# Hybrid diffusion backbone layer on one core: rows of h staged through the weight ring, layer-norm rows loaded one by one

## The chip, the core and the metric

The kernel runs on one core of a Trainium2 chip. The core has a matrix engine (PE in the profile; PEld is its weight load), a vector engine (DVE), a scalar engine (ACT), GpSimd (POOL) and a sync engine (SP), which here only issues DMAs. Each of them takes its own instructions strictly in the order in which they were put on its queue, and waits on semaphores for the others. 16 DMA engines move the data. The metric is the device time of one execution in microseconds; smaller is better.

## The reference, cut to what matters

One layer over 256 latent tokens `x` and 256 context tokens `ctx`, width 2048, all in float32:

```python
mod = silu(c) @ w_mod + b_mod;  shift, scale, gate = split(mod, 3)       # and the same for c_ctx
h   = layer_norm(x)   * (1 + scale)   + shift
h_c = layer_norm(ctx) * (1 + scale_c) + shift_c
aq, ak, av, az, bq, bk, bv, bz, bg, mga, mgb = split(h @ w_in)           # h_c: ak, av, bk, bv, bg are used
y_a = neighborhood_attention(aq, ak, av, ak_c, av_c, na_rpb)             # 16 heads of 64
y_b = gla(bq, bk, bv, bg, bk_c, bv_c, bg_c)                              # 4 heads, both directions
out = (sigmoid(mga) * ((y_a*silu(az)) @ w_br_a)
       + sigmoid(mgb) * ((y_b*silu(bz)) @ w_br_b)) @ w_out
x   = layer_norm(2**0.25 * x + gate * out, ln_g, ln_b)
```

## The kernel before, in words

**Number format.** Each factor of the big products is split into a high and a low part in the matrix engine's replicated float32 format (`split`, L146): ACT casts the high part (L148), DVE subtracts it from the source to get the low part (L150). Three matmuls (high x high, high x low, low x high) replace one.

**The weight ring.** All weights come as loads of 128 x 1024 numbers (512 KB; 352 KB for the value columns) through one tag of tiles, `raw`, with four buffers (`load`, L155, DMA at L157 on SP). A load's raw buffer is free again when its L150 has ended. The two parts go to tags `hi` and `lo` with three buffers each, which are free when the matmuls that read them are done. Two other things use the same four `raw` buffers: the position-bias tiles `rb` of the attention (L510, held from their fetch until both score blocks have added them), and the tiles `hr` with rows of h (L800, held until the four groups of matmuls that read them). Loads are counted from 1 in program order: loads 1 to 12 are aq0, aq1 (two each) and the eight value loads av0; 13 to 24 and 25 to 36 the same for the next two pairs of heads; 37 to 42 aq6, ak7, aq7; 43 to 50 bk and bq of the first GLA head.

**Rows of h.** The matrix engine needs h in two layouts. The transposed one is made at the start and stays on the chip (`hl`, tag of one buffer). The other one, token rows in two parts, is made in eight steps n = 0 to 7 (`rows_of_h`, L410) and stored to DRAM (`hrows`), from where `attended` reads it back as `hr` (L801). One step: SP loads the modulation columns, broadcast over the partitions, from DRAM `mods` into `sb` (L417) and rows of x into `xr` (L418); DVE makes h of them in eight instructions (four L423, four L424), ACT casts the high part into `sb`, DVE writes the low part over `xr` (L148, L150), SP stores both (L437). `sb` and `xr` are the two buffers of tag `staging`, so step n + 1 can't load before the stores of step n have ended. After step 6 in program order the tables `cs` and `wg` of the GLA stage take the same two buffers; `wg` is last read by the gates of head 3, `cs` by the rotation of its queries.

**What sets the order.** Program order is a priority. Steps hang on the loads as events (L444 to L451): the fetch of step n on load 6 + 6n, its cast and low part on the load behind it, its stores on load 11 + 6n. `tc.issue_after(ins)` puts an instruction behind `ins` on the queue of the engine of `ins`. A planner at build time walks through the program with estimated durations, gives out the buffers and writes each engine's fixed queue: an instruction whose buffer or input isn't there yet in its estimate lets later ones of the same engine pass.

**Attention's evacuation.** After the two query projections of a pair of heads, each 128 x 512 accumulator `qp` is emptied in eight short instructions that alternate between ACT (L495, L499) and DVE (L496, L500); the value projection `va` needs four accumulators of the same tag (`acc`, four buffers), so its third and fourth wait for the last L500 of either projection.

**The end.** When the last product that reads `hl` is done, its memory becomes `tail` (L1021): the rows of x, the layer-norm rows ln_g and ln_b (`fin`, four slices of 1 MB), the gate row and the results. The four slices are loaded by four DMAs on POOL's queue (L1033, L1034). The output projection `wo` runs in 24 loads (three column groups of eight) and a held last group; `turn` at the seventh load of the first group transposes the last quarter of the merged branches (`mt`, L934).

Of the kernel before, what the change touches and what calls it, by code (L numbers as in the profile page):

```python
# [8 lines left out]
F32 = mybir.dt.float32  # L9
# [7 lines left out]
P = 128  # L17
# [71 lines left out]
def tile_backbone_layer(  # L89
# [21 lines left out]
    nc = tc.nc  # L111
    const = ctx.enter_context(tc.tile_pool(name="const", bufs=1))
    hpool = ctx.enter_context(tc.tile_pool(name="hpool", bufs=1))
    stream = ctx.enter_context(tc.tile_pool(name="stream", bufs=3))
# [4 lines left out]
    mods = dram.tile([KT, 4, P], F32, name="mods")  # L119
# [11 lines left out]
    def acc(name):  # L131
        return ps.tile([P, 512], F32, tag="acc", name=name, bufs=4)
# [13 lines left out]
    def split(hi, lo, src, after=None):  # L146
        with tc.issue_after(after[0]) if after else nullcontext():
            cast = nc.scalar.copy(hi, src)  # L148
        with tc.issue_after(after[1]) if after else nullcontext():
            sub = nc.vector.tensor_tensor(out=lo, in0=src, in1=hi.bitcast(F32), op=ALU.subtract)  # L150
        return cast.ins, sub.ins

    loads, events = [], {}

    def load(src, n, name, after=None):  # L155
        raw = stream.tile([P, 1024], F32, tag="raw", name=f"r_{name}", bufs=4)
        dma = nc.sync.dma_start(raw[:, :n], src).ins  # L157
        hi = stream.tile([P, 1024], F32R, tag="hi", name=f"h_{name}")
        lo = stream.tile([P, 1024], F32R, tag="lo", name=f"l_{name}")
        cast, sub = split(hi[:, :n], lo[:, :n], raw[:, :n], after)  # L160
        loads.append((cast, sub))
        for event in events.pop(len(loads), ()):
            event(dma, sub)
        return hi, lo

    def unit(name, k):
        return load(wst[UNIT_AT[name, k]], 1024, f"{name}_{k}")
# [183 lines left out]
    for kt in range(KT):  # L351
# [3 lines left out]
        for p in range(K0):  # L355
# [3 lines left out]
            c = slice(P * p, P * p + P)  # L359
# [47 lines left out]
    def staging(shape, name, dt=F32R):  # L407
        return const.tile(shape, dt, tag="staging", name=name, bufs=2)

    def rows_of_h(n):  # L410
        sb = staging([P, 2, 4, P], f"sb{n}")
        xr = staging([P, 2, 4, P], f"xr{n}")
        b, x = sb[:].bitcast(F32), xr[:].bitcast(F32)

        def fetch_and_scale(dma, sub):
            with tc.issue_after(dma):
                nc.sync.dma_start(b, mods[2 * n : 2 * n + 2].partition_broadcast(P))  # L417
                nc.sync.dma_start(x, xrow[n])  # L418
            for i in range(4):
                xi, s = x[:, :, i, :], i // 2  # L420
                scale, shift = (b[:, :, 2 * m + s, :] for m in range(2))
                with tc.issue_after(sub):
                    nc.vector.scalar_tensor_tensor(xi, xi, mvs[:, i, 0:1], scale, ALU.subtract, ALU.mult)  # L423
                nc.vector.scalar_tensor_tensor(xi, xi, rsn[:, 0, i : i + 1], shift, ALU.mult, ALU.add)  # L424

        def parts(dma, sub):
            with tc.issue_after(sub):
                split(
                    sb[:].rearrange("p a b c -> p (a b c)"),
                    xr[:].rearrange("p a b c -> p (a b c)"),  # L430
                    x.rearrange("p a b c -> p (a b c)"),
                )

        def store(dma, sub):
            with tc.issue_after(dma):
                for part, src in enumerate((b, x)):
                    nc.sync.dma_start(  # L437
                        hrows[2 * n : 2 * n + 2, :, part].rearrange("f p j c -> p f (j c)"),
                        src.rearrange("p f a b -> p f (a b)"),
                    )  # L440

        return fetch_and_scale, parts, store

    for n in range(8):  # L444
        events.setdefault(6 + 6 * n, []).append(lambda dma, sub, n=n: rows_event(n, dma, sub))

    def rows_event(n, dma, sub):
        fetch, parts, store = rows_of_h(n)
        fetch(dma, sub)
        events.setdefault(7 + 6 * n, []).insert(0, parts)  # L450
        events.setdefault(11 + 6 * n, []).insert(0, store)  # L451
# [153 lines left out]
    for g in range(3):  # L605
# [4 lines left out]
        n = len(loads) + 1  # L610
# [13 lines left out]
    n = len(loads)  # L624
# [20 lines left out]
    lo = slice(64, 128)  # L645
# [283 lines left out]
    def turned(name, s, half):  # L929
        tp = bank(f"{name}_{half}")  # L930
        for i in range(2):
            for t in range(2):
                o = 256 * half + P * i
                nc.tensor.transpose(tp[:, T * i + P * t : T * i + P * t + P], s[:, t, o : o + P], ident[:])  # L934
        return tp
# [41 lines left out]
    def gated(c, which, ah, al, kt):  # L977
        g = rows_of(f"mg{which}{c}", xh, xl)
        s = k4([P, 2, 512], f"s{which}{c}")
        for t in range(2):  # L980
            sig = nc.scalar.activation(s[:, t, :], g[t][:], AF.Sigmoid)
        p = rows_of(f"p{which}{c}", ah, al, kt)
        for t in range(2):
            nc.vector.tensor_tensor(out=s[:, t, :], in0=s[:, t, :], in1=p[t][:], op=ALU.mult)
        return s, sig

    def turn(c, s):
        for half in range(2):
            tp = turned(f"mt{c}", s, half)
            a = 4 * c + 2 * half  # L990
            split(
                mhs[a // 8][:, a % 8 : a % 8 + 2, :].rearrange("p a b -> p (a b)"),
                mls[a // 8][:, a % 8 : a % 8 + 2, :].rearrange("p a b -> p (a b)"),
                tp[:],
            )
# [10 lines left out]
    for c in range(NC):  # L1006
# [5 lines left out]
        sb, sig = gated(c, "b", ybh, ybl, KT)  # L1012
# [9 lines left out]
    fin, gb, zs, zt0 = tail[:, 0:4], tail[:, 4], (tail[:, 5], tail[:, 6]), tail[:, 7]  # L1022
# [3 lines left out]
    for g in range(4):  # L1026
# [3 lines left out]
        mm(bp[:], ones_r[:], gh[:], True, False)  # L1030
        mm(bp[:], ones_r[:], gl[:], False, True)
        nc.scalar.copy(gb[:, 512 * g : 512 * g + 512], bp[:])
    for i, src in enumerate((xin[0], xin[1], lng.partition_broadcast(P), lnb.partition_broadcast(P))):  # L1033
        nc.gpsimd.dma_start(fin[:, i, :], src)  # L1034
    x_in, ln_g, ln_b = fin[:, 0:2], fin[:, 2], fin[:, 3]
    eps = tiny([P, 1], "eps", 1)
    nc.gpsimd.memset(eps[:], 1e-6)
# [4 lines left out]
    def out_mm(dst, wh, wl, a, t):  # L1042
        mh = mhs[a // 8][:, a % 8, P * t : P * t + P]
        ml = mls[a // 8][:, a % 8, P * t : P * t + P]
        mm(dst, mh, wh, a == 0, False)
        mm(dst, mh, wl, False, False)
        return mm(dst, ml, wh, False, a == KT - 1)

    def residual(op, t, n, lo, hi, scaled):
        cols = slice(lo, hi)  # L1050
        z = zs[t][:, cols]
        nc.vector.tensor_tensor(out=z, in0=op, in1=gb[:, cols], op=ALU.mult)
        nc.vector.scalar_tensor_tensor(z, x_in[:, t, cols], ALPHA, z, ALU.mult, ALU.add)
        nc.vector.bn_stats(sts[t][:, n, :], z)
        if scaled is not None:
            scaled.tensor_tensor(out=z, in0=z, in1=ln_g[:, cols], op=ALU.mult)

    for g in range(NC - 1):
        ops = [acc(f"wo{g}_{t}") for t in range(2)]
        for k in range(0, KT, 2):  # L1060
            if g == 0 and k == 12:
                turn(NC - 1, merged)
            wh, wl = unit(f"wo{g}", k)
            for t in range(2):
                for i in range(2):
                    c = slice(512 * i, 512 * i + 512)
                    out_mm(ops[t][:], wh[:, c], wl[:, c], k + i, t)
        for t in range(2):
            residual(ops[t][:], t, g, 512 * g, 512 * g + 512, nc.gpsimd)

    last = []
    for u in range(8):
        src = wst[UNIT_AT[f"wo{NC - 1}", 2 * u]]
        if u < HELD:
            raw = stream.tile([P, 1024], F32, tag="raw", name=f"r_last{u}", bufs=4)
# [4 lines left out]
        elif u == HELD:  # L1080
            raw = stream.tile([P, 1024], F32, tag="raw", name=f"r_last{u}", bufs=4)
# [163 lines left out]
```

## Time and profile before

| | us |
|---|---|
| median of 3 runs | 1234.91 (1233.46 to 1236.47) |
| the profiled execution's own time | 1236.99 |
| its span (first to last instruction) | 1235.3 |
| granted clock of the matrix engine, mean | 0.996 |
| bytes moved | 263.45 MB, mean 213 GB/s |

The profile's timeline gives, for each run of like instructions, the start, the time from the start of the first to the end of the last, the engine, the line and the operands; in brackets stands how long the engine was idle before it and on what it waited. A line of SP is the issue of a DMA. In the views by stage the columns are the busy time of PE, PEld, DVE, ACT and POOL with the number of instructions, the granted clock, the share of the DMA engines' time and GB/s.

### The profile page before, as it was taken

The numbers are of one execution on the slowest core, as the hardware profiler recorded it, in microseconds if no ns is written. First come the engines' busy times: TensorE is split into PE (matmuls) and PEld (weight loads), VectorE is DVE, ScalarE is ACT, GpSimd is POOL, SyncE is SP. The second block draws the span as 40 slices with busy tenths as digits, with TensorE's granted clock in tenths as the row PEclk, the third lists the DMA queues.
The fourth block names the chain that finished last, engine by engine and source line by source line (L and its number), as shares of the span: only waits on it lengthen the run. The fifth ranks groups of instructions, "written<-read, shape, count | busy, mean of one in ns | idle before, by whom it ended". The sixth has DMA issues, their size and how long they took to land.

```text
span 1235.3 us, 16298 instructions
## 1 busy us (share of the span) xinstructions
PE 1201.4 (97%) x6233; PEld 991.1 (80%) x6233; DVE 774.2 (63%) x1154; ACT 544.8 (44%) x776; POOL 65.9 (5%) x91
## 2 busy tenths in 40 slices
PE   6999999989999999999999999999999999999997
PEld 4666798979887887888888888888888888888785
DVE  6755677657759486355643466766566665665577
ACT  4322455545555354253532374544444444454341
POOL 1000100000001111001000000000000000000111
PEclk9999999999999999999999999999999999999999
DMA  9998566656743433543645567677776767657661
GB/s 372 417 404 308 160 199 187 201 169 189 237 144 109 135 126 130 188 153 120 238 165 189 213 226 233 231 235 239 238 247 230 241 237 241 227 187 268 215 216 68
DMA packets 77054, 263.45 MB, mean 213 GB/s; under 512 B 8920, under 2 KB 8936, under 8 KB 71856
## 3 DMA queue, kind: packets, MB, share of 16 engines
q1 hardware_dynamic: 73040, 252.49, 59.1%
q0 software_dynamic: 3504, 9.36, 2.7%
q8 instruction: 49, 0.80, 0.3%
q10 hardware_dynamic: 432, 0.56, 0.1%
q14 instruction: 29, 0.24, 0.1%
HBM read 247.66 MB, written 10.52 MB: 209 GB/s over the span
## 4 chain that ended last, share of the span: by engine, by line
PE 77%; DVE 10%; DMA 7%; ACT 2%; issue 2%; POOL 1%; SPq 0%; DVEq 0%; ACTq 0%
PE bz L144 7%; PE mgb L144 7%; PE pb L144 7%; PE mga L144 7%; PE kp L144 7%; PE o L144 7%; PE bk L144 6%; PE g L144 6%; PE va L144 5%; PE pa L144 4%; PE az L144 2%; PE bq L144 2%; PE gp L144 2%; PE qp L144 2%; PE wo L144 2%
## 5 line engine op out<-in xcount | busy, mean ns | idle before, releaser
L144 PE MATMUL va<-h_av,hl 128*128 128x352 f32 x384 | 97.6, 329 | 7.5 <-DVE q L500 7.5
L144 PE MATMUL kp<-hl,h_ak 128*128 128x512 f32 x256 | 86.7, 406 | 2.3 <-ACT hl L305 2.3
L144 PE MATMUL o<-h_wv,gt 128*128 128x512 f32 x256 | 84.0, 390 | 0.9 <-ACT gt L148 0.6
L144 PE MATMUL bk<-hl,h_bk 128*128 128x512 f32 x256 | 80.8, 392 | 0.7 <-ACT kf L690 0.7
L144 PE MATMUL bz<-h_bz,hl 128*128 128x512 f32 x256 | 80.6, 392 | 0.0
L144 PE MATMUL g<-ah,hr 128*128 128x512 f32 x256 | 79.3, 390 | 0.8 <-DVE sga L855 0.8
L144 PE MATMUL mgb<-h_mgb,hl 128*128 128x512 f32 x256 | 79.8, 390 | 0.0
L144 PE MATMUL mga<-h_mga,hl 128*128 128x512 f32 x256 | 79.5, 389 | 0.0
L144 PE MATMUL pb<-h_pb,hl 128*128 128x512 f32 x256 | 79.4, 389 | 0.0
L150 DVE TENSOR_TENSOR l_wv<-r_wv,h_wv 128x1024 fp32r<-128x1024 f32 x32 | 39.7, 1239 | 63.4 <-ACT h_wv L148 63.2
L144 PEld LDWEIGHTS va<-h_av,hl 128*128 128x128 f32 x384 | 68.2, 191 | 10.0 <-issue 9.6
L150 DVE TENSOR_TENSOR l_pb<-r_pb,h_pb 128x1024 fp32r<-128x1024 f32 x32 | 39.2, 1225 | 39.9 <-ACT h_pb L148 39.9
L144 PEld LDWEIGHTS kp<-hl,h_ak 128*128 128x128 f32 x256 | 47.8, 189 | 19.1 <-issue 5.3
L144 PE MATMUL va<-l_av,hl 128*128 128x352 f32 x192 | 62.2, 324 | 0.0
L148 ACT CAST h_wv<-r_wv 128x1024 fp32r<-128x1024 f32 x32 | 33.6, 1050 | 57.7 <-DMA r_wv<-in_wst 57.6
L150 DVE TENSOR_TENSOR l_mgb<-r_mgb,h_mgb 128x1024 fp32r<-128x1024 f32 x32 | 39.2, 1225 | 30.1 <-ACT h_mgb L148 29.9
L144 PEld LDWEIGHTS o<-h_wv,gt 128*128 128x128 f32 x256 | 48.0, 188 | 11.6 <-ACT gt L148 1.0
L144 PEld LDWEIGHTS bk<-hl,h_bk 128*128 128x128 f32 x256 | 48.1, 188 | 11.3 <-ACT kf L690 1.1
L144 PEld LDWEIGHTS g<-ah,hr 128*128 128x128 f32 x256 | 47.8, 188 | 10.9 <-DVE sga L855 1.2
L150 DVE TENSOR_TENSOR l_mga<-r_mga,h_mga 128x1024 fp32r<-128x1024 f32 x32 | 39.2, 1224 | 27.5 <-ACT h_mga L148 27.5
L144 PEld LDWEIGHTS pb<-h_pb,hl 128*128 128x128 f32 x256 | 48.1, 188 | 10.0
L144 PEld LDWEIGHTS mga<-h_mga,hl 128*128 128x128 f32 x256 | 48.1, 188 | 10.0
(338 smaller groups left out, 2967.2 us busy)
## 6 DMA issues: line engine op xcount, KB each, us to landing
wm<-in_wmod SPq DMA_DIRECT2D x32, 1024.0 KB, 9.1
hr<-hrows SPq DMA_DIRECT2D x32, 512.0 KB, 4.2
r_wv<-in_wst SPq DMA_DIRECT2D x32, 512.0 KB, 3.5
r_bz<-in_wst SPq DMA_DIRECT2D x32, 512.0 KB, 4.1
wg<-in_wgate SPq DMA_DIRECT2D x64, 256.0 KB, 3.7
r_mga<-in_wst SPq DMA_DIRECT2D x32, 512.0 KB, 3.8
r_mgb<-in_wst SPq DMA_DIRECT2D x32, 512.0 KB, 3.3
r_pb<-in_wst SPq DMA_DIRECT2D x32, 512.0 KB, 3.3
```

The lines of the kernel that those rows point to most:

```text
L144: return nc.tensor.matmul(o, a, b, start=start, stop=stop).ins
L148: cast = nc.scalar.copy(hi, src)
L150: sub = nc.vector.tensor_tensor(out=lo, in0=src, in1=hi.bitcast(F32), op=ALU.subtract)
```

## The change

Step n's x rows and modulation columns become tiles of tag `raw`, so they take two of the ring's four buffers; x is now loaded ahead of the modulation columns. The two `staging` buffers take only the high and the low part, from the cast on. The four slices of `fin` are no longer loaded on POOL in one go but on SP, one behind each of the loads 1, 3, 5 and 7 of the first `wo` group.

```diff
     def rows_of_h(n):
-        sb = staging([P, 2, 4, P], f"sb{n}")
-        xr = staging([P, 2, 4, P], f"xr{n}")
-        b, x = sb[:].bitcast(F32), xr[:].bitcast(F32)
+        def home(name):
+            return stream.tile([P, 2, 4, P], F32, tag="raw", name=f"{name}{n}", bufs=4)
+
+        x, b = home("xr"), home("sb")
+        hi, lo = staging([P, 2, 4, P], f"rh{n}"), staging([P, 2, 4, P], f"rl{n}")
 
         def fetch_and_scale(dma, sub):
             with tc.issue_after(dma):
-                nc.sync.dma_start(b, mods[2 * n : 2 * n + 2].partition_broadcast(P))
-                nc.sync.dma_start(x, xrow[n])
+                nc.sync.dma_start(x[:], xrow[n])
+                nc.sync.dma_start(b[:], mods[2 * n : 2 * n + 2].partition_broadcast(P))
...
         def parts(dma, sub):
             with tc.issue_after(sub):
-                split(
-                    sb[:].rearrange("p a b c -> p (a b c)"),
-                    xr[:].rearrange("p a b c -> p (a b c)"),
-                    x.rearrange("p a b c -> p (a b c)"),
-                )
+                split(*(t[:].rearrange("p a b c -> p (a b c)") for t in (hi, lo, x)))
 
         def store(dma, sub):
             with tc.issue_after(dma):
-                for part, src in enumerate((b, x)):
+                for part, src in enumerate((hi, lo)):
                     nc.sync.dma_start(
                         hrows[2 * n : 2 * n + 2, :, part].rearrange("f p j c -> p f (j c)"),
-                        src.rearrange("p f a b -> p f (a b)"),
+                        src[:].rearrange("p f a b -> p f (a b)").bitcast(F32),
                     )
...
-    for i, src in enumerate((xin[0], xin[1], lng.partition_broadcast(P), lnb.partition_broadcast(P))):
-        nc.gpsimd.dma_start(fin[:, i, :], src)
+    fins = [xin[0], xin[1], lng.partition_broadcast(P), lnb.partition_broadcast(P)]
+
+    def fetch_fin(i):
+        events.setdefault(len(loads) + 1, []).append(lambda dma, sub: fetch_fin_at(i, dma))
+
+    def fetch_fin_at(i, dma):
+        with tc.issue_after(dma):
+            nc.sync.dma_start(fin[:, i, :], fins[i])
+
...
             if g == 0 and k == 12:
                 turn(NC - 1, merged)
+            if g == 0 and k in (0, 4, 8, 12):
+                fetch_fin(k // 4)
             wh, wl = unit(f"wo{g}", k)
```

## The prediction

> **What bounds the kernel now.** I read the page's busy shares first, then the matrix engine's timeline for every idle gap, and then, stage by stage, who ends it.
>
> ```profile
> PE 1201.4 (97%) x6233; PEld 991.1 (80%) x6233; DVE 774.2 (63%) x1154; ACT 544.8 (44%) x776; POOL 65.9 (5%) x91
> ```
>
> PE is busy for 1201.4 of 1235.3 us, so all its idle time together is 34 us, and most of that lies before the first and behind the last big product. The gaps that the edits can reach, from PE's timeline and, in the last line, from the waits between 140 and 345 us:
>
> ```profile
> 212.74 0.40 PE L144 MATMUL va<-h_av,hl 128*128 128x352 f32 x1 [1.80 <-DVE q L500]
> 265.31 0.40 PE L144 MATMUL va<-h_av,hl 128*128 128x352 f32 x1 [1.12 <-DVE q L500]
> 270.88 0.63 PE L144 MATMUL va<-h_av,hl 128*128 128x352 f32 x1 [3.68 <-DVE q L500]
> 592.54 0.50 PE L144 MATMUL o<-l_wv,gt 128*128 128x512 f32 x1 [0.53 <-DVE l_wv L150]
> 1149.03 0.99 PE L144 MATMUL wo<-h_wo,mh 128*128 128x512 f32 x3 [1.97 <-ACT h_wo L148]
> PE va L144 <- DVE q L500: 7.5, 5, 3.7
> ```
>
> So the stake is small: 7.5 us where `va` waits for the emptying of `qp` (steps 0, 2 and 4 of the rows of h fall there), 0.5 us around step 7, 2.0 us at the end. One gap costs more than its length; the stretches behind the 3.68 us one:
>
> ```profile
> 271.00:274.00 3.00, 3.00 (x10) 2.90 (x11) 0.56 (x1) 0.78 (x1) 0.00 (x0) 0.50 0.24 94
> 274.00:277.00 3.00, 3.00 (x20) 3.00 (x20) 2.06 (x3) 0.84 (x3) 0.00 (x0) 0.97 0.35 84
> ```
>
> The granted clock is 0.50 for 3 us, with 10 matmuls instead of 20: another 1.5 us lost. All in reach is then about 11.5 us, 0.9%. The Trainium skill ("TensorE: Matmul & The Clock Gate", Part 1: The HAM clock gate) says that the clock falls to half after about one idle window of 3.4 us and needs as much busy time to come back; by that, each gap that the change pushes past that length costs some 1.7 us more. This trace agrees, with 3.68 us idle and 0.50 granted.
>
> **The change, steps 0 to 6.** What goes is the wait of step n's loads on the stores of step n - 1 (SP's own waits):
>
> ```profile
> SPq L417 <- DMA hrows<-sb: 11.1, 6, 3.2
> SPq L418 <- DMA hrows<-xr: 7.0, 6, 2.3
> ```
>
> What comes is two more tenants in the ring. A ring buffer is free when its load's L150 ends, so after the change x of step 4 takes the buffer of load 28, the modulation columns that of load 29, and load 31, on SP behind both, that of load 30. SP's, DVE's and ACT's lines around step 4:
>
> ```profile
> 250.72 1.22 DVE L150 TENSOR_TENSOR l_aq<-r_aq,h_aq 128x1024 fp32r<-128x1024 f32 x1
> 254.55 0.89 DVE L150 TENSOR_TENSOR l_av<-r_av,h_av 128x704 fp32r<-128x704 f32 x1
> 256.58 0.89 DVE L150 TENSOR_TENSOR l_av<-r_av,h_av 128x704 fp32r<-128x704 f32 x1 [0.82 <-ACT h_av L148]
> 251.39 0.33 SPq L417 DMA_DIRECT2D sb<-mods  x1
> 254.00 0.33 SPq L418 DMA_DIRECT2D xr<-in_xrow  x1
> 254.43 3.40 SPq L157 DMA_DIRECT2D r_av<-in_wav  x3
> 261.93 0.88 DVE L423 SCALAR_TENSOR_TENSOR xr<-xr,mvs,sb 128x256 f32<-128x256 f32 x2 [4.01 <-issue]
> 263.52 0.78 ACT L148 CAST h_av<-r_av 128x704 fp32r<-128x704 f32 x1 [4.64 <-DMA r_av<-in_wav]
> r_av<-in_wav SPq DMA_DIRECT2D x24, 352.0 KB, 4.8
> ```
>
> DVE stands idle for 4.01 us before its first L423, until x is there (254.00 + 7.9), and ACT for 4.64 us until load 31 is there (254.43 + 9.1). The L496/L500 and L495/L499 of the evacuation are queued behind these two, and `va` waits for them: that is the 4.8 us of gaps. New issue times: x 251.9 (2.1 us earlier), modulation columns 255.4 (4.0 later), load 31 257.5 (3.0 later). With landings between the 4.8 us that is the median of the value loads (last row, from the DMA issues) and the 9.1 us above, I take 6.5, since less traffic stands ahead of them: the columns land at 261.9, load 31 at 264.0. So the same two instructions wait about as long as before, -1.6 to +3.1 us (columns landing in 4.8, load 31 in 9.1).
>
> Step 2 the same way:
>
> ```profile
> 199.66 0.89 DVE L150 TENSOR_TENSOR l_av<-r_av,h_av 128x704 fp32r<-128x704 f32 x1
> 201.70 0.89 DVE L150 TENSOR_TENSOR l_av<-r_av,h_av 128x704 fp32r<-128x704 f32 x1 [0.82 <-ACT h_av L148]
> 196.22 0.33 SPq L417 DMA_DIRECT2D sb<-mods  x1
> 197.42 0.33 SPq L418 DMA_DIRECT2D xr<-in_xrow  x1
> 197.85 5.09 SPq L157 DMA_DIRECT2D r_av<-in_wav  x3
> 203.85 0.88 DVE L423 SCALAR_TENSOR_TENSOR xr<-xr,mvs,sb 128x256 f32<-128x256 f32 x2 [0.81 <-DMA xr<-in_xrow]
> 205.36 0.78 ACT L148 CAST h_av<-r_av 128x704 fp32r<-128x704 f32 x1 [1.37 <-DMA r_av<-in_wav]
> ```
>
> Columns at 200.6 instead of 196.2, load 19 at 202.6 instead of 197.85. Landing 6 us later they let L423 start at 206.6 (+2.7) and the cast at 208.6 (+3.2). Step 0 has no wait now; load 7 moves from 147.11 to the end of load 6's L150:
>
> ```profile
> 151.28 0.89 DVE L150 TENSOR_TENSOR l_av<-r_av,h_av 128x704 fp32r<-128x704 f32 x1 [0.84 <-ACT h_av L148]
> 147.11 5.42 SPq L157 DMA_DIRECT2D r_av<-in_wav  x3
> 153.52 0.78 ACT L148 CAST h_av<-r_av 128x704 fp32r<-128x704 f32 x1
> ```
>
> 152.2 + 5 = 157.2 against a cast at 153.52: +3.7. If the queues of ACT and DVE keep their order, the three steps cost +3.7 + 3.2 + 0.5 = +7.4 us at the last L500, and PE, which has no slack there, all of it. The planner knows about the buffers, however: with the loads later in its estimate it lets evacuation instructions pass ahead of the L423s and the cast. If it lets all of them pass, the 7.5 us and the 1.5 us of slow clock go: -9. Between these ends I take +2, nearer to the middle: two hops of the evacuation (some 0.9 us each, 1.8 in all) passing ahead at each of the three steps gives 7.4 - 5.4 = +2.0. Steps 1, 3, 5 and 6 I cost at nothing: their loads are aq, ak and bk, issued ten us and more ahead of use; that cover gone, a step would cost the 2 us that step 2 does.
>
> **Step 7** has its loads now where the GLA tables free the staging buffers, and its eight L423/L424 in the busiest stretch of DVE there:
>
> ```profile
> 579.22 0.33 SPq L418 DMA_DIRECT2D xr<-in_xrow  x1
> 591.27 1.22 DVE L150 TENSOR_TENSOR l_wv<-r_wv,h_wv 128x1024 fp32r<-128x1024 f32 x1
> ```
>
> The first also shows that the planner lets a load without a buffer be passed: step 7 hangs on load 48, a bq load. After the change x and columns are loaded near 345 us and scaled there, and only cast, low part and stores wait for the staging buffers, until about 583; eight instructions leave the queue ahead of L150 at 591.27, on which PE waits 0.53: -0.6 (0 to -1.5). But x then keeps one of four ring buffers from about 345 to 580 us. Where `hr` and weights alternate, the weights have one buffer:
>
> ```profile
> 488.02 0.33 SPq L157 DMA_DIRECT2D r_wv<-in_wst  x1
> 493.55 0.33 SPq L157 DMA_DIRECT2D r_wv<-in_wst  x1
> 497.66 2.72 PE g L144 x12
> 500.38 2.72 PE o L144 x12
> ```
>
> One buffer turns round in 5.53 us, PE needs a load every 5.44. The third buffer of `hr` can go (two leave it 8.2 us from issue to use); the weights start later and with less lead. I take +0.3; 0 to +5 (0.6 us for each of eight loads, if the lead is gone).
>
> **The end.** POOL's four 1 MB loads start at 1128.4 and share the DMA engines with the weights:
>
> ```profile
> 1128.37 1.08 POOL L1034 DMA_DIRECT2D tail<-in_xin  x2 [57.98 <-PE gb L144]
> 1134.24 3.75 SPq L157 DMA_DIRECT2D r_wo<-in_wst  x2
> 1147.93 1.04 ACT L148 CAST h_wo<-r_wo 128x1024 fp32r<-128x1024 f32 x1 [2.46 <-DMA r_wo<-in_wst]
> 1135.00:1140.00 5.00, 5.00 (x24) 4.14 (x23) 2.09 (x2) 2.11 (x2) 0.00 (x0) 1.00 1.01 410
> ```
>
> The load issued at 1137.7 lands at 1147.9; its cast starts then, and PE goes on at 1149.03. On SP, slices 1 to 3 can go when `hl` is free, at 1128.4, slice 4 behind the seventh weight load. At the 410 GB/s of the last row a slice takes 2.6 us and a weight load 1.3; in one queue the critical load has four slices and two loads ahead of it: 1128.4 + 2 (start and landing) + 4 x 2.6 + 3 x 1.3 = 1144.7, and its cast is done by 1145.8, ahead of PE. Gain 2.0 if so, 0 if the mean rate stays that of before; I take -1.6. Should SP hold slice 1 in program order, right behind the first `wo` load, five weight loads would queue behind a wait until 1128.4 and PE would lose some 4 us and win 2: +2. The Trainium skill ("DMA: Bandwidth & Descriptors", Queues, rings and completion order) says that one queue is consumed in order and that two take turns by packets. Read strictly it speaks against the move, each weight load standing behind whole slices; the landing of 10.2 us beside POOL's queue agrees with the taking of turns, and no run yet shows the other half.
>
> **Sum.** +2.0 - 0.6 + 0.3 - 1.6 = +0.1 us on the profiled execution's 1236.99. That execution lies 2.1 us above the median of 1234.91; put on the median, the forecast is 1235.0.
>
> **Rivals.** A measurement of this kernel can tell about 0.2%, 2.5 us, from no change. *Evacuation unhindered:* steps 2 and 4 no longer hold the L496 to L500; half of the 9 us and the 1.9 of the other terms give 1228.5, all of it 1224. For it: the removed store waits of 18.1 us. Against: load 31 lands no earlier. Chance 0.28. *Slower, load behind the two new tenants:* the cast of loads 7, 19 and 31 stays where it is in ACT's queue and holds the L499s: +7.4 - 1.9 = 1240.5, and 1242 with one more slow-clock stretch; it decides as soon as load 19 lands after about 206.5 and its cast still precedes the evacuation. For it: the 1.37 and 4.64 us waits stand at this cast already. Chance 0.25. *Ring of three in the GLA stage:* +5 there, 1240. Chance 0.06. *Not doing what it says at the end:* slice 1 waits in program order; 2.0 in place of -1.6, 1238.6. Chance 0.04. The forecast, no difference that can be measured (1232.4 to 1237.4): 0.37.
>
> Chances: faster 0.28, same 0.37, slower 0.35. The range is 1229 to 1243: full relief and the sum of two bad cases are left out, about 0.2.
>
> **What will show it.** PE's gaps behind DVE L500 near 155 to 165, 205 to 215 and 260 to 275 us, with the first L423 and the ACT cast ahead of them: their idle time against 4.01, 0.81, 4.64 and 1.37. SP's issue of load 19 against 202.6 and of the columns against 200.6. The slices' order on SP, the landing of the weight load issued near 1137.7 (under 8 us for me) and the 1.97 us gap gone. Step 7's x loaded near 345 us. Wrong would make it above all a queue order on ACT or DVE that I did not foresee.

## The result and the profile after

The changed kernel takes 1256.4 us in the median of four runs (1255.54 to 1257.42), the kernel before on the same chip 1235.69 (1233.46 to 1238.37): a ratio of 1.0167, 95% interval 1.0144 to 1.0190. It is 20.7 us slower where 1235.0 was forecast, and outside the range of 1229 to 1243. The profiled execution took 1255.54, its span 1253.8.

The busy share of the matrix engine on the page of the kernel after:

```profile
PE 1211.8 (97%) x6233; PEld 996.4 (79%) x6233; DVE 773.4 (62%) x1154; ACT 545.2 (43%) x776; POOL 64.2 (5%) x87
```

It is the same 97% as before, so this line does not show the loss: PE is busy 10.4 us more with the same matmuls and idle 8.1 us more. I therefore divide the span at four landmarks of PE's stream that every kernel has, each the start of a matmul: the first `ap` (the near scores of the GLA stage; the matmuls with `near` alone), the last `bk` and the last `az` (projections in that stage) and the first `wo` (the h_bk, h_az and h_wo matmuls). In us:

| kernel (profiled execution) | to first ap | to last bk | to last az | to first wo | to the end | span |
|---|---|---|---|---|---|---|
| before | 424.4 | 140.3 | 164.5 | 399.3 | 106.8 | 1235.3 |
| after | 425.9 | **153.6** | **171.3** | 399.3 | 103.7 | 1253.8 |
| e_fin | 424.6 | 140.0 | 164.3 | 399.3 | 103.6 | 1231.8 |
| e_rows | 429.5 | 153.0 | 171.4 | 399.3 | 105.1 | 1258.3 |
| e_old67 | 422.2 | 139.9 | 165.0 | 399.3 | 103.7 | 1230.1 |
| e_old6 | 422.8 | 140.8 | 166.0 | 399.4 | 103.9 | 1232.9 |
| e_dum2 | 425.8 | **150.1** | 165.7 | 399.3 | 109.3 | 1250.2 |
| e_dum1 | 424.1 | 140.4 | 166.8 | 399.3 | 106.3 | 1236.9 |
| e_late | 424.8 | 140.3 | **176.4** | 399.3 | 106.0 | 1246.8 |
| e_old067 | 420.9 | 140.5 | 165.0 | 399.4 | 103.8 | 1229.6 |
| e_five | 422.7 | 140.3 | 164.3 | 399.3 | 104.5 | 1231.1 |
| e_five4 | 427.3 | 140.3 | 163.1 | 399.3 | 104.1 | 1234.1 |
| e_oldfive | 421.1 | 140.0 | 163.4 | 399.3 | 103.6 | 1227.4 |

Each row is one execution. after and e_rows are the same kernel up to the first `wo` and still differ by 3.6 us at the first `ap`, but by at most 0.6 in the next two columns; so a few us in the first column are no reading.

The loss has two places: 13.3 us between the first `ap` and the last `bk` (426 to 580 us) and 6.8 us behind it. The end gained 3.1, and all that lies ahead of the first `ap`, where the prediction spent most of its words, lost 1.5, no more than such chance. The views by stage of before and of after (columns as above):

```profile
455.00:545.00 90.00, 88.40 (x433) 74.17 (x432) 46.47 (x86) 40.38 (x59) 5.94 (x7) 1.00 0.50 168
580.00:625.00 45.00, 44.47 (x224) 37.70 (x223) 29.89 (x64) 24.95 (x42) 0.53 (x1) 1.00 0.57 199
```

```profile
455.00:545.00 90.00, 82.37 (x380) 65.78 (x379) 45.57 (x92) 38.80 (x57) 6.51 (x7) 0.96 0.41 140
580.00:625.00 45.00, 40.60 (x190) 33.49 (x189) 24.66 (x44) 16.79 (x24) 4.67 (x6) 0.92 0.57 186
```

In the same 90 us PE issues 380 matmuls instead of 433, and DMA moves 140 GB/s instead of 168: PE starves, and the DMA engines, busy for 0.41 of the time, are not the limit. Why stands in the issues of SP, first of before, then of after; POOL's loads of the table `cs` follow, in the same order:

```profile
334.18 0.43 SPq L437 DMA_DIRECT2D hrows<-sb  x1
334.66 1.03 SPq L437 DMA_DIRECT2D hrows<-xr  x1
```

```profile
310.74 0.34 SPq L419 DMA_DIRECT2D xr<-in_xrow  x1
...
348.51 0.33 SPq L419 DMA_DIRECT2D xr<-in_xrow  x1
...
506.90 0.37 SPq L435 DMA_DIRECT2D hrows<-rh  x1
...
594.89 0.38 SPq L435 DMA_DIRECT2D hrows<-rl  x1
595.97 0.38 SPq L435 DMA_DIRECT2D hrows<-rh  x1
597.74 0.33 SPq L799 DMA_DIRECT2D hr<-hrows  x1
599.48 0.36 SPq L435 DMA_DIRECT2D hrows<-rl  x1
```

```profile
342.90 0.55 POOL L643 DMA_DIRECT2D cs<-in_rope  x1 [10.12 <-DMA hrows<-xr]
```

```profile
313.80 0.58 POOL L641 DMA_DIRECT2D cs<-in_rope  x1 [7.39 <-DMA hrows<-rl]
```

In the kernel before, step 6 is stored at 334 us and `cs` comes after it. In the kernel after, `cs` comes at 313.80, as soon as the stores of step 5 free a staging buffer, and `wg`, written by ACT at 338.9, takes the other one. Step 6 asks for staging only at its cast, and finds none: its high part is stored at 506.90, its low part at 594.89, and step 7's parts at 595.97 and 599.48. So x of step 6 (loaded at 310.74) and x of step 7 (348.51) both stay in the weight ring until then. Two consequences follow: the ring has two buffers instead of four, and rows 12 to 15 of h, which `hr` reads, come to DRAM at 597 us and later.

### The profile page after: what moved, and what is told of

The parts are those of the page before. It is cut to its first block, busy times and chain, and to the rows that moved or that the text cites. A ratio compares the mean times of both kernels' runs of the same rounds, so it can differ in the third digit from the quotient of the medians.

```text
span 1253.8 us, 16294 instructions
## 1 busy us (share of the span) xinstructions
PE 1211.8 (97%) x6233; PEld 996.4 (79%) x6233; DVE 773.4 (62%) x1154; ACT 545.2 (43%) x776; POOL 64.2 (5%) x87
## 4 chain that ended last, share of the span: by engine, by line
PE 79%; DVE 8%; DMA 7%; ACT 3%; issue 2%; POOL 0%; SPq 0%; DVEq 0%; ACTq 0%; POOLq 0%
PE bz L144 7%; PE mgb L144 7%; PE va L144 7%; PE pb L144 7%; PE mga L144 7%; PE kp L144 7%; PE bk L144 7%; PE g L144 5%; PE o L144 5%; PE pa L144 3%; PE wo L144 3%; DMA r_wv<-in_wst 3%; PE az L144 3%; PE bq L144 2%; PE qp L144 2%; PE gp L144 2%
## 5 line engine op out<-in xcount | busy, mean ns | idle before, releaser
L144 PE MATMUL g<-ah,hr 128*128 128x512 f32 x256 | 82.4, 403 | 3.9 <-DMA hr<-hrows 3.2
L150 DVE TENSOR_TENSOR l_wv<-r_wv,h_wv 128x1024 fp32r<-128x1024 f32 x32 | 39.1, 1224 | 67.0 <-ACT h_wv L148 66.9
L150 DVE TENSOR_TENSOR l_pb<-r_pb,h_pb 128x1024 fp32r<-128x1024 f32 x32 | 39.2, 1225 | 39.9 <-ACT h_pb L148 39.9
L150 DVE TENSOR_TENSOR l_mgb<-r_mgb,h_mgb 128x1024 fp32r<-128x1024 f32 x32 | 39.2, 1225 | 30.1 <-ACT h_mgb L148 29.9
L150 DVE TENSOR_TENSOR l_mga<-r_mga,h_mga 128x1024 fp32r<-128x1024 f32 x32 | 39.2, 1224 | 27.5 <-ACT h_mga L148 27.5
```

The costliest lines, as they stand in the source:

```text
L144: return nc.tensor.matmul(o, a, b, start=start, stop=stop).ins
```

## The experiments

The theory from this profile: the loss is steps 6 and 7, through the short ring and the late rows. Rivals: steps 0 to 5 in the ring and the new queue orders cost it; `fin` on SP costs it; one of the two consequences costs all.

### The parts alone

**e_fin**: the kernel before with the `fin` part of the diff only.

> The kernel before with the change at the end alone: the four slices of fin on SP behind wo loads 1, 3, 5 and 7; rows of h as before. Theory (the end's gain is its own, about 3.3 us of PE's lead between the first wo matmul and the last gap): 3.3 us below before, about 1232.4, with the 1.97 us gap behind the ACT cast of h_wo gone. Rival (the gain in the changed kernel came from the 20 us by which everything ahead was later, not from the queue): within 1 us of before, the gap still there.

Measured 1233.39 us, ratio to before 0.9981 (0.9967 to 0.9994). The end is 3.2 us shorter in the profile, and the move is worth about 2.2 us by itself. One line of PE, then SP's issues, in e_fin:

```profile
1146.93 0.50 PE L144 MATMUL wo<-h_wo,mh 128*128 128x512 f32 x1 [0.24 <-ACT mh L148]
```

```profile
1127.49 0.90 SPq L1040 DMA_DIRECT2D tail<-in_xin  x2
1128.43 0.43 SPq L1040 DMA_DIRECT2D tail<-in_lng  x1
1130.64 0.33 SPq L157 DMA_DIRECT2D r_wo<-in_wst  x1
1131.01 0.44 SPq L1040 DMA_DIRECT2D tail<-in_lnb  x1
```

Where the kernel before waited 1.97 us for a cast of `h_wo`, there is now 0.24 us behind `mh`, the merged branches. The slices go as soon as `hl` is free, three in a row, and the weights do not stand behind them long enough to stop PE.

**e_rows**: the other half of the diff, with `fin` on POOL as before.

> The changed kernel with fin loaded on POOL as before: rows of h through the ring alone. Theory (the rows carry the whole loss): 3.3 us above the changed kernel, about 24 us above before, 1259.7. Rival (fin on SP takes part in the loss): not above the changed kernel.

Measured 1259.01, ratio 1.0180 (1.0160 to 1.0201): the rows carry the whole loss, some 23 us.

### Which steps

**e_old67** and **e_old6**: the changed kernel with the old `rows_of_h` for some steps:

```diff
+    def rows_of_h(n):
+        return rows_old(n) if n >= 6 else rows_new(n)        # e_old6: n == 6
```

> The changed kernel, but steps 6 and 7 use staging for x and columns as before; steps 0 to 5 through the ring, fin on SP. Theory (the loss is steps 6 and 7: two ring buffers kept over the GLA stage, and rows 12 to 15 of h stored only at 595 to 600 us): the whole loss goes, steps 0 to 5 are worth about -0.9 us, the end -3.3: about 1231.5, and no ring buffer is held by x between 355 and 590 us. Rival (tenants of steps 0 to 5, or the other queue orders that the planner makes of them, carry it): 1240 or more.

> The changed kernel, but step 6 alone uses staging as before, so that cs and wg get it only when the parts of step 6 are stored; x of step 7 still stays in one ring buffer from about 350 to 595 us. This is the case that the prediction's ring term priced (+0.3, 0 to +5). Theory, strong form (a ring of three is nearly free, the second buffer and the late rows carry the loss): 1231.5 to 1236. Rival (each tenant costs its half of the 13.3 us that went in 455 to 545 us): about 1240, with gaps behind loads of l_wv in that stage.

e_old67 measured 1232.13, ratio 0.9970 (0.9957 to 0.9983): 24 us come back with two of eight steps, and the changed steps 0 to 5 cost nothing (1.3 us below e_fin, and the two intervals overlap). The rival that steps 0 to 5 carry the loss falls. e_old6 measured 1235.79, ratio 1.0001 (0.9987 to 1.0015). There only x of step 7 stays in the ring, which is the schedule that the prediction had in mind, and the time, 1235.79, is near the one that it gave, 1235.0. That is luck: the terms measured here are -1.3 for steps 0 to 5, -2.2 for the end and +3.7 for step 7 with its ring of three, where it had +2.0, -1.6 and -0.3. Against e_old67 it costs 3.7 us: the upper end of what the theory allowed, and little more than half of what the rival's share of 13.3 would be. By the table only 0.9 of it falls between the first `ap` and the last `bk`.

### The ring alone

**e_dum2** and **e_dum1** leave the rows of h of the kernel before as they are and only take ring buffers away:

```diff
+        d = stream.tile([P, 2, 4, P], F32, tag="raw", name=f"dm{len(held)}", bufs=4)
+        with tc.issue_after(dma):
+            nc.sync.dma_start(d[:], xrow[0])                  # at loads 42 and 48; e_dum1: 48
...
+                with tc.issue_after(last.ins):                # behind the rotation of head 3's queries
+                    nc.vector.tensor_copy(tiny([P, 1], f"dt{i}", 1)[:], d[:, 0, 0, 0:1])
```

> The kernel before, with two extra tiles of tag raw: loaded from xrow at loads 42 and 48, as x of steps 6 and 7 is in the changed kernel, and released by a copy of one column behind the rotation of head 3's queries. Rows of h, their stores and fin as before; only the ring is short by two from about 350 to 590 us. Theory (two causes: ring of two, and rows 12 to 15 late): the ring's share alone, the 13.3 us that went between 455 and 545 us and 1 to 3.7 around it: 1249 to 1253. Rival 1 (all of it is the ring): 1257 or more. Rival 2 (all of it is the late rows): within 2 us of before.

> As the kernel with two extra tiles, but only the one loaded at load 48: a ring of three from about 350 to 590 us. Theory (the price is steep: nothing for the first buffer, all for the second, since one buffer alternating with hr turns round in about PE's own 5.4 us and none to spare costs the rest): 1235.5 to 1239, the 3.7 us between the two kernels with and without x of step 7 in the ring being the upper end. Rival (each buffer costs its half): about 1243.

e_dum2 measured 1250.28, ratio 1.0118 (1.0092 to 1.0144), in the theory's 1249 to 1253; e_dum1 1239.30, ratio 1.0024 (1.0010 to 1.0037). The first tenant costs 3.3 us, the second 11 more in the medians. In the table 9.8 of e_dum2's 14.9 us fall between first `ap` and last `bk`, where e_dum1 loses 0.1; 2.5 fall in the end, long after the tenants are gone, where the `fin` loads on POOL still meet the weights: the gap there is 2.70 us in this execution, and PE runs at half clock for 3.4 us behind it. That share is not the ring's; without it the second tenant costs some 9 us, by these two profiles.

The 9.8 are less than the 13.3 of the kernel after, with the same two buffers gone. The difference is mostly the clock: after has two stretches of 3.4 us at half clock in this stage (from 477.6 and from 518.6), e_dum2 has none, although its gaps at the same two places are 1.96 and 1.56 us, against 2.46 and 1.54. Half of the 6.8 us, an estimate, added to the 9.8 makes 13.2. The sum holds to about 1 us: e_rows, with 12.7 us lost here and one such stretch, comes to 11.0 in place of 9.8.

The mechanism shows in one turn of the loop of `g` and `o` in the kernel after (PE, SP, ACT and DVE in order of time):

```profile
523.55 0.63 PE L144 MATMUL g<-ah,hr 128*128 128x512 f32 x2
...
524.43 0.32 SPq L799 DMA_DIRECT2D hr<-hrows  x1
...
524.85 0.39 SPq L157 DMA_DIRECT2D r_wv<-in_wst  x1
...
528.31 0.73 PE L144 MATMUL g<-ah,hr 128*128 128x512 f32 x2 [1.18 <-DMA hr<-hrows]
...
529.54 1.05 ACT L148 CAST h_wv<-r_wv 128x1024 fp32r<-128x1024 f32 x1 [4.51 <-DMA r_wv<-in_wst]
...
530.62 1.23 DVE L150 TENSOR_TENSOR l_wv<-r_wv,h_wv 128x1024 fp32r<-128x1024 f32 x1 [4.87 <-ACT h_wv L148]
...
531.37 0.32 SPq L799 DMA_DIRECT2D hr<-hrows  x1
...
531.88 0.33 SPq L157 DMA_DIRECT2D r_wv<-in_wst  x1
```

With two buffers, one is the weight's and one is `hr`'s. The next `hr` can be loaded only when the `g` matmuls have read the last one (524.43, as they end); it lands 3.8 us later, and PE has only 2.7 us of `o` to do in between, so it waits 1.18. Then `g` takes 2.9, and the next load goes at 531.37: 6.9 us for a turn in which PE has 5.44 of work. The weight's buffer turns as slowly: issued at 524.85, cast at 529.54, low part done at 531.85, next issue at 531.88, 7.0 us, since its data come in behind those of `hr`: 4.7 us after issue, against 3.2 to 3.3 in the loop of before. The four `hr` issues from 524.43 to 544.49 are 6.7 us apart, against the 5.44 that PE needs. In the kernel before, `hr` had lead and only the weight stood in a single buffer, at 5.53 us a turn; the prediction reckoned with that loop.

Who held the `hr` issue between 455 and 550 us, SP's own waits in before, after, e_dum2 and e_old6:

```profile
SPq L801 <- PE g L144: 9.2, 8, 4.3
```

```profile
SPq L799 <- PE g L144: 29.2, 9, 5.9
```

```profile
SPq L817 <- PE g L144: 29.2, 9, 4.6
```

```profile
SPq L836 <- PE g L144: 6.8, 7, 2.2
```

The waits for `g` are three times as long with two buffers, by whatever tenant, and not longer with three. With three buffers one stream still has a lead; with two neither has, so the price is a step and not a slope.

### The late rows alone

**e_late**: step 6 of the kernel before stores to a second DRAM tile, which is copied to rows 12 and 13 of `hrows` behind the rotation of head 3's queries:

```diff
+                        (early[:, :, part] if n == 6 else hrows[2 * n : 2 * n + 2, :, part]).rearrange("f p j c -> p f (j c)"),
...
+            nc.sync.dma_start(hrows[12, :, 0, 0, :], qr[:, 0, 0:P])
+            nc.sync.dma_start(
+                hrows[12:14].rearrange("f p a b c -> (f p) (a b c)"),
+                early[:].rearrange("f p a b c -> (f p) (a b c)"),
+            )
```

The small write of `qr` is overwritten by the copy; it only makes the copy wait for the rotation.

> The kernel before, but step 6 stores to another DRAM tile and its rows (12 and 13) are copied to hrows only behind the rotation of head 3's queries, some 590 to 600 us, about when the changed kernel stores them. The ring is as before. Theory (two causes): the 7.0 us that went between 580 and 613 us in the changed kernel, 1240 to 1244. Rival (all of it is the ring): within 2 us of before.

Measured 1248.41, ratio 1.0097 (1.0073 to 1.0121), more than expected. By the table 11.9 us go between last `bk` and last `az` and none in the ring's stage: so late rows do cost there, with the ring of before. SP and PE in e_late:

```profile
580.00 0.33 SPq L720 DMA_DIRECT2D hrows<-qr  x1
583.19 0.56 SPq L721 DMA_DIRECT2D hrows<-early  x1
588.40 0.34 SPq L805 DMA_DIRECT2D hr<-hrows  x1
```

```profile
586.95 0.80 PE L145 MATMUL ap<-near 128*128 128x128 f32 x2 [4.69 <-DVE near L750]
...
592.66 1.19 PE L145 MATMUL g<-ah,hr 128*128 128x512 f32 x2 [2.44 <-DMA hr<-hrows]
```

The size is overstated. Row 12 is fetched at 588.40, where the kernel before does it at 568.51: 19.9 us late. In the kernel after it is 597.74, with all work ahead 14.8 us later, so 14.4 us late; and the copy also holds SP and the weights behind it. The same place in the kernel after, PE and DVE:

```profile
596.19 0.39 PE L144 MATMUL o<-h_wv,gt 128*128 128x512 f32 x1
600.21 0.58 PE L144 MATMUL ap<-near 128*128 128x128 f32 x2 [3.63 <-DVE near L743]
```

```profile
593.64 1.23 DVE L150 TENSOR_TENSOR rl<-xr,rh 128x1024 fp32r<-128x1024 f32 x1
...
598.23 1.22 DVE L150 TENSOR_TENSOR rl<-xr,rh 128x1024 fp32r<-128x1024 f32 x1
...
599.73 0.76 DVE L743 TENSOR_TENSOR near<-kr,cc 128x256 f32<-128x256 f32 x2
```

PE has finished row 11, row 12 isn't there, and all that is left is head 3's `near`, for which DVE has yet to make the two low parts that came late. A reader of the gap alone would blame `near`; the `near` instructions are no slower than before, they are only no longer covered. Nor are they late: the first starts at 599.36, in the kernel before at 586.04, which with the 14.8 us of delay ahead would be 600.8. PE is idle 3.7 us more than before between last `bk` and last `az`; behind the gap it runs at half clock until 607.3 us, which costs some 3 us (an estimate, half of the time that PE is busy from 600.5 to 607.3). How much earlier `near` would come without the two L150 ahead of it was not measured.

### Repairs, and the best version

**e_old067** keeps step 0 in staging too, since the gaps at 157 and 163 us stood there in e_old67 (2.39 and 0.89 us, against 0.36 and 0.49):

> The changed kernel, but steps 0, 6 and 7 use staging for x and columns as before; steps 1 to 5 through the ring, fin on SP. Theory (step 0 in the ring costs the gaps of 2.39 and 0.89 us in front of va at 157 and 163 us, which are 0.36 and 0.49 with step 0 in staging): 2.4 us below the kernel with steps 0 to 5 in the ring, about 1229.7. Rival (the planner gives it back in the next steps): 1232.

Measured 1232.11, ratio 0.9963 (0.9949 to 0.9978). The two gaps are back at 0.36 and 0.49 us, but the time is that of e_old67, as the rival said. Its reason is seen in part: the gap of step 2 grows from 1.73 to 2.21 us, and 3.4 us at half clock follow it (from 212.7), of which e_old67 has none.

**e_five** and **e_five4** keep the change whole, and only hang the steps closer, so that step 7 is through staging before the tables ask for it; **e_oldfive** does that to the old scheme with `fin` on SP:

```diff
-        events.setdefault(6 + 6 * n, []).append(lambda dma, sub, n=n: rows_event(n, dma, sub))
+        events.setdefault((6 + 5 * n), []).append(lambda dma, sub, n=n: rows_event(n, dma, sub))
...
-        events.setdefault(7 + 6 * n, []).insert(0, parts)
-        events.setdefault(11 + 6 * n, []).insert(0, store)
+        events.setdefault((6 + 5 * n) + 1, []).insert(0, parts)
+        events.setdefault((6 + 5 * n) + 5, []).insert(0, store)   # e_five4: + 4
```

> The changed kernel with its rows of h, all eight through the ring, hung on every fifth load (6 + 5n, parts one load later, stores five later) instead of every sixth, so that step 7 is cast and stored before the tables cs and wg come to the staging buffers. Theory (the loss is who gets staging first, not the ring as a home): the loss of some 24 us goes, no x stands in the ring after about 345 us, all rows are in DRAM by then, cs is loaded after the stores of step 7: 1229 to 1234. Rival (the ring as a home for x and columns costs, now beside the bias tile rb in the attention stage): above 1240.

> The same with the stores four loads behind the fetch instead of five. Theory: as the other within 2 us, 1229 to 1234. Rival (SP held by a store whose low part is not written yet, weights behind it): 3 us or more above the other, with a gap of PE behind a weight load in the attention stage.

> Control: the kernel before with fin on SP, x and columns in staging as before, but the steps on every fifth load too. If the early step 7 is what counts, and not the home of x: as the two kernels above, within 2 us. If the store waits of staging make the denser steps impossible without holding the evacuation: 3 us or more above them.

| kernel | us | ratio to before | 95% interval |
|---|---|---|---|
| e_five | 1232.32 | 0.9971 | 0.9959 to 0.9983 |
| e_five4 | 1235.96 | 1.0000 | 0.9987 to 1.0014 |
| e_oldfive | 1229.76 | 0.9958 | 0.9945 to 0.9972 |

The stores of the eight steps in e_five (first and last start), and then POOL's load of `cs`:

```profile
L435 SPq DMA_DIRECT2D hrows<-rh x8: 426/430/567, 168.7 to 330.2; - x8
```

```profile
338.94 0.55 POOL L641 DMA_DIRECT2D cs<-in_rope  x1 [9.01 <-DMA hrows<-rh]
```

All eight steps are stored by 331 us, `cs` comes behind them, and the 24 us are gone with the ring still the home of x and columns. With e_old67 that settles the cause: it is who gets the staging buffers first, not the ring as a home. e_oldfive is the best of all, 5.2 us below before (0.9958 of 1235.7) and 2.6 below e_five, though their intervals overlap: with every step early, the ring as a home for x and columns gains nothing over staging. e_five4 is 3.6 us above e_five, which is its rival's price, but the rival's sign is not there: in the attention stage PE waits no more than 0.4 us behind a weight load in either. The profiled e_five4 comes to the first `ap` 4.6 us later; its idle time is about the same, and it has two stretches of 3.4 us at half clock (from 268.1 and 319.3) where e_five has none, some 3.4 of the 4.6 us. Why twelve runs are slower in the median stays open.

## Why the prediction was wrong

**What bounds the kernel, and the stake.** Right that PE is the bound and has 34 us of idle time; wrong to conclude that only the gaps already there were at stake. A change that takes a resource can open new ones.

**Steps 0 to 6, +2.0 (-9 to +7.4).** For steps 0 to 5 e_old67 against e_fin gives -1.3, no difference that can be told. The +2.0 lies within 3.3 of it by luck more than by working: it is a point between +7.4 and -9, set by two hops for each step that no row showed. The mechanism was seen half. The SP issues were foreseen in their distances: x, columns and load 31 of step 4 (255.92, 259.42 and 261.46) came 3.5 and 2.0 us apart, as worked out, all 4 us later than given. The planner did let evacuation pass ahead of the cast, and the gaps of `va` behind DVE, from PE's timeline of the kernel after, became these:

```profile
157.01 0.63 PE L144 MATMUL va<-h_av,hl 128*128 128x352 f32 x1 [2.47 <-DVE q L498]
...
214.65 0.58 PE L144 MATMUL va<-h_av,hl 128*128 128x352 f32 x1 [1.88 <-DVE q L498]
...
271.04 0.43 PE L144 MATMUL va<-h_av,hl 128*128 128x352 f32 x1 [1.72 <-DVE q L498]
```

Step 0 lost (0.36 before), step 2 kept its 1.8, step 4 gained (1.12 and 3.68 with its slow stretch became 1.72): 6.1 us in all against 7.5. At each of the first two of these gaps a stretch of 3.4 us at half clock begins, in before at one gap only: some 1.7 us more (an estimate, half of 3.4), by which the 1.4 us are spent again. The rival "evacuation unhindered" and the rival "cast behind the two tenants" both didn't come.

**Step 7 and the ring: the step that failed.** The prediction says that "x then keeps one of four ring buffers", and that only step 7's parts wait for the tables. It took step 6 as served first, the order in which step 6, `cs` and `wg` stand in the program, and gave no reason. But a staging buffer is now asked for by the cast, and the tables are ready earlier: `cs` waits for nothing but a buffer. The trace of before held the sign, in the row of POOL shown above: `cs` waited 10.12 us for the stores of step 6, so its load stood ready at 332.8 us, ahead of their issue at 334.18. I had not asked who else wants the buffer that the change leaves empty from the stores of one step to the cast of the next. A ring of three was priced at +0.3 (0 to +5) and -0.6 for step 7; e_old6 and e_dum1 measured +3.7 and +3.3 for that case, inside the bounds and mis-sized by some 3 us. A ring of two and late rows were in no rival and in no end of the range, and those cost the 20 us: 13.3 in the ring's stage and 6.8 behind it.

**The end, -1.6 (-2.0 to 0, or +2).** Right: -2.2 in e_fin (-0.7 to -4.1 by the interval), the 1.97 us gap gone, three slices issued as `hl` came free, the fourth behind the next weight load, no block of SP in program order. One sign was missed by little: the weight load issued near 1137 us landed 8.3 us after issue in e_fin, not under 8, against 10.2 in before. The rule of the Trainium skill ("DMA: Bandwidth & Descriptors", Queues, rings and completion order) that one queue is consumed in order fits the two weight loads behind the slices, which landed 9.9 and 10.4 us after issue, where the one just ahead of them took 3.5. But beside POOL's queue, in before, the same two took 9.6 and 10.1, so these runs do not tell the order in the queue from the mere sharing of the DMA engines; PE had the lead for either.

**Slow clock.** The prediction gave it 1.5 us, and more only for a gap past 3.4 us. From 100 us on PE runs at half clock in five places of the kernel after: for 3.4 us each from 156.7, 214.8, 477.6 and 518.6, and for 6.8 us from 600.5; in before once, for 3.4 us from 270.7. Half of the time that PE is busy in them is the estimate of the price: 3.4 of the 13.3 us and some 3 of the 6.8. The means in the views by stage, 0.96 over 90 us and 0.92 over 45, give 3.6 in each. Four of the five follow gaps of 1.54 to 2.47 us.

## What to carry to other kernels

When a tile moves to another buffer, ask of each buffer it leaves and enters who else wants it and when the new first writer asks: a buffer that is claimed later can go to a rival that is ready earlier, as it did here against the program order. A row in the trace in which that rival waits for the buffer is the warning. And price a ring by the buffers that stay free in the tightest loop: the loss of the first cost 3 us here, that of the second some 9 to 11 more, since with one buffer for each of two alternating streams a load can only start when its consumer has ended.

## What the runs showed of the hardware

The clock did not follow the length of a gap alone. Three stretches of the kernel after, behind gaps of 2.46, 1.54 and 3.63 us (at 477.30, 517.95 and 600.21), and the one behind the gap of 3.01 us at 213.90 in e_five:

```profile
477.50:480.50 3.00, 3.00 (x11) 2.52 (x11) 3.00 (x12) 0.74 (x2) 0.00 (x0) 0.52 0.54 175
...
518.00:521.00 3.00, 3.00 (x8) 2.38 (x9) 1.79 (x7) 0.63 (x1) 0.00 (x0) 0.59 0.48 175
...
603.20:607.20 4.00, 4.00 (x10) 3.10 (x10) 0.00 (x0) 0.00 (x0) 0.00 (x0) 0.50 0.90 353
```

```profile
213.90:216.90 3.00, 3.00 (x17) 2.83 (x18) 0.87 (x1) 0.78 (x1) 0.00 (x0) 1.00 0.75 296
```

The granted clock was halved after 1.54 us of idle time and stayed at 1.00 after 3.01; behind the longest gap it was still 0.50 three us later. The prediction's rule of one idle window of 3.4 us (the Trainium skill, "TensorE: Matmul & The Clock Gate", Part 1: The HAM clock gate) is thus too simple for this trace.

The same section calls that window free-running, and here the trace agrees. Read in steps of 0.1 us, the clock of the kernel after falls at 156.74, 214.77, 477.60, 518.56 and 600.48 us. These lie 58.03, 262.83, 40.96 and 81.92 us apart, which is 17, 77, 12 and 24 times 3.413; and each slow stretch lasts one such step, the last one two. So the falls stand on a fixed grid, as with a window that is judged step by step. How much idle time in a step is enough stays open: in the steps that ended with these falls PE was idle 2.20, 1.88, 2.46, 1.54 and 3.14 us, but e_dum2, whose falls at 213.71 and 271.73 place its own grid, kept its clock at 1.00 after the step from 514.07 to 517.49, which holds the whole of its 1.56 us gap.
